# A state-space layer and an attention layer on one core: the first input stretch, and when group 0's y is made

## The chip, the cores and the metric

The kernel runs on one core of a Trainium2 chip. The metric is the device time of one execution in microseconds; before the change it is 840.81 us, the median of three runs (840.78 to 840.98). The engines are PE (matrix products, with the weight loads as PEld), DVE (vector), ACT (scalar functions and casts), POOL (not used here beyond four constants) and SP, whose queue issues nearly all loads.

## The reference, cut to what matters

Two layers with residuals and a final norm, on 512 tokens of width 1024. The change lies in the first layer, the state-space mixer:

```python
proj = u @ in_w                      # u = rms_norm(x); 1024 -> 2048 (z) + 4096 (x, B, C) + 32 (dt)
xbc = silu(causal_depthwise_conv(xbc, conv_w, conv_b))
dt = softplus(dt_raw + dt_bias)
a = dt * (-exp(a_log))
y = ssd_chunked(xs * dt, a, b_in, c_out)     # 8 groups of 4 heads, chunks of 128 tokens
y = y + d_skip * xs
y = gated_group_rms_norm(y, z, norm_w, 8)
return y @ out_w
```

The scan of one group and chunk (t, s are tokens of the chunk) is

```python
cb = C B^T ;  y_diag = (cb * exp(a_cum[t] - a_cum[s]), causal) @ xdt
states = B^T (decay_to_end * xdt), carried from chunk to chunk
y_off = exp(a_cum) * (C @ entering_state)
```

The second layer is latent attention with 16 heads. It is not touched.

## The kernel before, in words

Channels lie on the partitions and the 512 tokens along the free side. Every fp32 operand of a large product is split into a high part and the rest (whi and wlo for weights, vh and vl or ah and al for activations), and a product is three passes: vh with whi, vl with whi, vh with wlo. One projection tile (128 output channels) takes 8 input tiles x 3 = 24 matmuls of 128x512. ACT casts the high part (L272, L398, L311), DVE subtracts it for the rest (L273, L402, L312).

A weight tile is 512 KB. It is loaded on SP's queue into one of two raw buffers (L263), and split into one of three whi and three wlo buffers; the order of the tiles is a list (wq), and a load is issued as soon as its raw buffer is free.

The first layer projects for each of 8 groups six tiles in the order B, C, x0, x1, z0, z1. The projections of group g+1 run on PE while the scan of group g is fed in between. The generator ssm_in yields a cost after every six matmuls and one more at the end of a tile (6 x 0.216 = 1.296 each); `sched` adds these up and calls a piece of other work as soon as the sum reaches the piece's number. The tables S0P, SU, P0 (group 0), P1 (groups 1 to 7) and GN hold these numbers, and PE's order is the order of these calls. On the other engines a scheduler sets the order when the program is built.

The steps that the prediction names:

- *First stretch.* The input x comes in eight tiles (L376), the first two weight tiles in four quarters each between them (L381). B and C of group 0 run in step (gemm2, L300): for each input tile three matmuls of B and three of C. Input is not yet normed there: products use x times the norm's weight, and the norm's factor (rr) is applied to the results.
- *The norm of the input* (norm0, sumsq, L342 to L357, L223, L322 to L324): squares on ACT, sums on DVE, sqh and sql, two products with ones (pssq), logarithm, exponential, and three DVE steps to rr.
- *dt* (ssm_dt): 16 products (L495, L496); the product with rr (d, L500) and four transposes (L504); softplus by a series on DVE; then the second half: cumulative sum by a product (L540), its copy acT (L544) and exponential to DRAM (ac_d, ea_d), transposes of acT (L553), and two more products (L558, L559).
- *The scan of a group* (class SSD): lexp loads four L tiles, broadcast from ac_d (L627), and takes their exponentials; cb (L71 to L81), x for each half (L89 to L94, xdt and xw), states (L105 to L113), y (L123 to L148: loads of E from ea_d, products yo at L130 and yd at L138, and eight DVE steps).
- *The norm of y* (gnorm, sumsq again): for group g it is called in the projections of group g+2, at GN.
- *Convolution and SiLU* of B, C, x0, x1 (L606 to L613): per tile one ACT step and three DVE steps.

Of the kernel before, what the change touches and what calls it, by code (L numbers as in the profile page):

```python
# [50 lines left out]
OA = 8  # L51
SQ = 2


# [97 lines left out]
class Net:  # L152
# [113 lines left out]
    def split_weight(self, raw, cuts=()):  # L266
# [28 lines left out]
    def gemm2(self, ps, ws, xh, xl, ks):  # L295
        seqs = [self.passes(w, xh, xl, ks) for w in ws]
        for k in range(ks):
            for p, seq in zip(ps, seqs):
                for i in range(3 * k, 3 * k + 3):
                    self.nc.tensor.matmul(p, seq[i][0], seq[i][1], start=i == 0, stop=i == 3 * ks - 1)  # L300
            yield 6 * 0.216

# [34 lines left out]
    def sumsq(self, tiles, n, pstag, pool=None, tags=("r0", "rt", "rr"), after=None):  # L337
        nc = self.nc
        acc = None
        for x in tiles:  # L340
# [19 lines left out]
    def ssm(self):  # L360
# [9 lines left out]
        self.link(self.head, [ld])  # L370
        self.phase, self.group = "E", [self.head]
        raws = [self.wraw.tile([P, D], F32, tag="raw", name=self.nm("raw")) for _ in range(2)]
        self.wload = 2
        for k in range(KD):
            x = self.res.tile([P, T], F32, tag="res", name=self.nm("x"))
            nc.sync.dma_start(x[:], t["x"][k])  # L376
            self.xs.append(x)
            if k % 2 == 0:
                s = slice(k * P, (k + 2) * P)
                for i, raw in enumerate(raws):  # L380
                    nc.sync.dma_start(raw[:, s], t["w"][i, :, s])  # L381
        wdt = wk.tile([P, KD, NH], F32, name="wdt", bufs=1)
# [9 lines left out]

        vh, vl = [], []
        ws = [self.split_weight(raw, (256, 512, 768)) for raw in raws]
        for k in range(KD):
            a = self.o16.tile([P, T], F32R, tag="o", name=self.nm("vh"))
            b = self.o16.tile([P, T], F32R, tag="o", name=self.nm("vl"))
            last = nc.scalar.activation(a[:], self.xs[k][:], AF.Copy, scale=nw[:, k:k + 1])  # L398
            if k % 2 == 0:
                for w in ws:  # L400
                    next(w)
            nc.vector.scalar_tensor_tensor(b[:], self.xs[k][:], nw[:, k:k + 1], a[:].bitcast(F32), op0=ALU.mult,  # L402
                                           op1=ALU.subtract)
# [4 lines left out]
        self.wpos = 2  # L408
# [24 lines left out]
        for g in range(NG):  # L433
            ys, q = [], []
            pieces = [] if g == 0 else [(GN, late)]
            if g == 0:
                begin = lambda: q.append(SSD(self, 0, self.lexp(0), ys))
                pieces += [(SU[0] + SU[1] * k, scaled) for k in range(KD)]
                pieces += [(P0[0], step), (P0[1], step), (P0[1] + 0.1, begin)]
                at = P0[2:]  # L440
            else:
                q.append(SSD(self, g, self.lexp(g), ys))
                at = P1
            pieces += [(at[0], lambda: q[0].cb()), (at[1], lambda: q[0].x(0)), (at[2], lambda: q[0].x(1)),
                       (at[3], lambda: q[0].states()), (at[4], lambda: q[0].y())]
            if g + 1 < NG:
# [118 lines left out]
    def ssm_in(self, g, uh, ul, early):  # L565
# [3 lines left out]
        for i, (name, ct) in enumerate((("B", 16 + g), ("C", 24 + g), ("x0", 2 * g), ("x1", 2 * g + 1),  # L569
                                        ("z0", 0), ("z1", 0))):  # L570
            pair = (0, 1) if g == 0 and i < 2 else (4, 5) if g == NG - 1 and i >= 4 else None
            w = None if pair and i == pair[1] else self.weight("w", U_IN + 6 * g + i)
            xh, xl, r = early[:3] if i < early[3] else (uh, ul, None)
# [4 lines left out]
            if pair:  # L578
                if i == pair[0]:
                    two = [ps, self.mm()]  # L580
                    ws = [w, self.weight("w", U_IN + 6 * g + i + 1)]
                    yield from self.gemm2([p[:] for p in two], ws, xh, xl, KD)
# [489 lines left out]
```

## Time and profile before

The profiled execution took 840.15 us, and the span from its first to its last instruction is 838.3 us.

| engine | busy us | share of the span | instructions |
|---|---|---|---|
| PE | 822.8 | 98% | 4260 |
| PEld | 694.8 | 83% | 4260 |
| DVE | 640.2 | 76% | 1226 |
| ACT | 453.5 | 54% | 802 |

The chain that ended last is 91% PE and 5% DVE. A row of a timeline reads: start in us, duration in us, engine, line, operation, output and inputs by the program's names without numbers, shapes, how many equal ones; in brackets the engine's idle time before it and what ended it. Matmuls overlap, so the distance of two starts is what one takes, not its duration. A row of waits reads: who waited, for whom: us in total, times, longest.

### The profile page before, as it was taken

Reading aid. Unit: us, or ns where it says so; the run is one execution under the profiler, and the core shown is the slowest. Engines: PE = TensorE matmul, PEld = TensorE weight load, DVE = VectorE, ACT = ScalarE, POOL = GpSimd, SP = SyncE. Lnnn points to the kernel's source line nnn. Section 1 sums busy time; section 2 is a strip of 40 time slices with the busy share of each in tenths; the row PEclk is TensorE's granted clock in tenths of the full one; section 3 lists DMA queues with packets and bytes.
Section 4 is the critical chain, followed back from the end, with each engine's and each line's share of the span. In section 5 each row is a group of like instructions: output and inputs, shape, how many; then the busy total and the mean of one; then the engine's idle time right before and its main releaser. Section 6 shows DMA issues by size and latency. Waiting matters only on the chain.

```text
span 838.3 us, 11586 instructions
## 1 busy us (share of the span) xinstructions
PE 822.8 (98%) x4260; PEld 694.8 (83%) x4260; DVE 640.2 (76%) x1226; ACT 453.5 (54%) x802; POOL 0.2 (0%) x4
## 2 busy tenths in 40 slices
PE   7999999999999999999999999999999999999996
PEld 5887888888888888888888888888888888888885
DVE  7899898979788979776564887786767869675544
ACT  7567755545565657333354664456547557554233
POOL 0000000000000000000000000000000000000000
PEclk9999999999999999999999999999999999999999
DMA  6354543434242424323225242222221224331212
GB/s 227 102 186 145 153 150 106 147 101 128 98 151 76 151 87 137 121 95 101 90 86 176 79 129 64 77 65 73 73 64 56 89 75 157 100 100 53 92 59 100
DMA packets 35112, 90.55 MB, mean 108 GB/s; under 512 B 4784, under 2 KB 6320, under 8 KB 35056
## 3 DMA queue, kind: packets, MB, share of 16 engines
q1 hardware_dynamic: 34336, 88.77, 32.9%
q10 hardware_dynamic: 720, 1.05, 0.3%
q8 instruction: 33, 0.54, 0.3%
q14 instruction: 23, 0.19, 0.1%
HBM read 83.12 MB, written 4.33 MB: 104 GB/s over the span
## 4 chain that ended last, share of the span: by engine, by line
PE 91%; DVE 5%; DMA 2%; ACT 1%; issue 1%; SPq 0%; DVEq 0%; ACTq 0%
PE mm L291 54%; PE ot L942 11%; PE s L794 5%; PE mm L300 4%; PE po L836 4%; PE mm L774 3%; PE pt L818 2%; PE yd L138 2%; PE yd L291 1%; PE aux L130 1%; PE aux L105 1%; DMA x<-in_x_dram 1%; PE aux L77 1%; PE aux L89 1%; DMA L<-ac_d 1%; DVE wlo L273 1%
## 5 line engine op out<-in xcount | busy, mean ns | idle before, releaser
L272 ACT CAST whi<-raw 128x1024 fp32r<-128x1024 f32 (+3 forms) x132 | 127.0, 965 | 214.7 <-PE mm L291 177.4
L273 DVE TENSOR_TENSOR wlo<-raw,whi 128x1024 fp32r<-128x1024 f32 (+3 forms) x132 | 146.8, 1115 | 56.1 <-ACT whi L272 55.8
L291 PE MATMUL mm<-ah,whi 128*128 128x512 f32 x384 | 153.9, 401 | 0.0
L291 PE MATMUL mm<-ah,wlo 128*128 128x512 f32 x384 | 150.1, 391 | 0.4 <-DVE wlo L273 0.4
L291 PE MATMUL mm<-al,whi 128*128 128x512 f32 x384 | 149.8, 390 | 0.0
L291 PE MATMUL mm<-vh,whi 128*128 128x512 f32 x224 | 89.6, 400 | 0.9 <-ACT whi L272 0.9
L291 PE MATMUL mm<-vh,wlo 128*128 128x512 f32 x224 | 87.8, 392 | 0.7 <-DVE wlo L273 0.7
L291 PE MATMUL mm<-vl,whi 128*128 128x512 f32 x224 | 87.5, 391 | 0.0
L291 PEld LDWEIGHTS mm<-ah,wlo 128*128 128x128 f32 x384 | 72.1, 188 | 16.0 <-DVE wlo L273 0.8
L291 PEld LDWEIGHTS mm<-ah,whi 128*128 128x128 f32 x384 | 72.2, 188 | 15.5 <-issue 1.4
L291 PEld LDWEIGHTS mm<-al,whi 128*128 128x128 f32 x384 | 72.2, 188 | 14.4 <-DVE al L312 0.3
L942 PE MATMUL ot<-whi,ah 128*128 128x512 f32 (+1 forms) x136 | 52.3, 384 | 0.0
L942 PE MATMUL ot<-whi,al 128*128 128x512 f32 (+1 forms) x136 | 51.4, 378 | 0.0
L942 PE MATMUL ot<-wlo,ah 128*128 128x512 f32 (+1 forms) x136 | 51.4, 378 | 0.0
L291 PEld LDWEIGHTS mm<-vh,wlo 128*128 128x128 f32 x224 | 42.0, 188 | 10.8 <-DVE wlo L273 1.5
L291 PEld LDWEIGHTS mm<-vh,whi 128*128 128x128 f32 x224 | 42.1, 188 | 9.2 <-ACT whi L272 1.1
L223 ACT ACTIVATE p<-p,st 128x128 f32<-128x128 f32 (+1 forms) x64 | 36.1, 564 | 25.1 <-DVE st L806 25.0
L291 PEld LDWEIGHTS mm<-vl,whi 128*128 128x128 f32 x224 | 42.2, 188 | 7.2
L822 ACT CAST ph<-pt 128x512 fp32r<-128x512 f32 (+1 forms) x64 | 26.5, 422 | 33.2 <-PE pt L818 32.8
L291 PE MATMUL mm<-ch,whi 128*128 128x512 f32 x104 | 42.6, 409 | 0.0
L291 PE MATMUL mm<-ch,wlo 128*128 128x512 f32 x104 | 40.8, 392 | 0.0
L291 PE MATMUL mm<-cl,whi 128*128 128x512 f32 x104 | 40.7, 392 | 0.0
(225 smaller groups left out, 1642.6 us busy)
## 6 DMA issues: line engine op xcount, KB each, us to landing
raw<-in_w_dram SPq DMA_DIRECT2D x100, 512.0 KB, 3.3
L<-ac_d SPq DMA_DIRECT2D x32, 256.0 KB, 3.8
E<-ea_d SPq DMA_DIRECT2D x32, 128.0 KB, 3.3
raw<-in_ua_dram SPq DMA_DIRECT2D x8, 512.0 KB, 3.3
raw<-in_ub_dram SPq DMA_DIRECT2D x8, 320.0 KB, 2.9
x<-in_x_dram SPq DMA_DIRECT2D x8, 256.0 KB, 4.3
res<-in_x_dram SPq DMA_DIRECT2D x8, 256.0 KB, 3.3
hd<-ht SPq DMA_DIRECT2D x8, 256.0 KB, 2.3
```

What stands on the lines that cost most here:

```text
L138: nc.tensor.matmul(yd[64 * h:64 * h + 64, s], self.xdt[j][:, c, h, :], self.L[2 * j + h][:, s], start=True, stop=True)
L223: i = self.nc.scalar.activation(out, in_, func, **k)
L272: nc.scalar.copy(hi[:, a:b], raw[:, a:b])
L273: nc.vector.tensor_tensor(lo[:, a:b], raw[:, a:b], hi[:, a:b].bitcast(F32), op=ALU.subtract)
L291: self.nc.tensor.matmul(ps, a, b, start=i == 0, stop=i == len(seq) - 1)
L300: self.nc.tensor.matmul(p, seq[i][0], seq[i][1], start=i == 0, stop=i == 3 * ks - 1)
L774: nc.tensor.matmul(ps[:, c2 * 256:(c2 + 1) * 256], a, b, start=i == 0, stop=i == 5)
L794: nc.tensor.matmul(ps[:, :n], x[:, s], y[:, :n], start=k == 0, stop=k == 4)
L818: nc.tensor.transpose(pt[:, (b - kb) * P:(b - kb + 1) * P], probs[h][b][:, kb * P:(kb + 1) * P], self.ident)
L822: nc.scalar.copy(ph[:, :n], pt[:, :n])
L836: nc.tensor.matmul(po[:, kb * P:], x, y, start=kb == 0 and k == 0, stop=kb == NCH - 1 and k == 2)
L942: nc.tensor.matmul(ps[:, a:b], x, y, start=start and i == 0, stop=stop and i == 5)
```

## The change

Four things change.

1. Ahead of everything PE multiplies a tile of zeros by itself eight times (WARM = 8).
2. x0 of group 0 joins B and C in the first stretch: three weight tiles are loaded in quarters between the input tiles, split by split_first, and gemm2 makes nine matmuls for each input tile. The third raw tile lies in two buffers of the pool of ah and al. The squares of the norm are tied to the input tiles three places on, so that they run inside the stretch.
3. S0P: dt's first products, the norm and the flush come right behind the stretch, and dt's transposes behind 12 matmuls of x1 (21.9). P0: dt's second half at 10.4 and 11.2 instead of 6.0 and 6.8, and cb, x0, x1 and states of group 0 later.
4. Group 0's y is no longer called in group 0, but at PL = 5.0 in group 1; group 1's own scan starts (lexp) at 5.1, and its pieces follow a table of their own, PM. GN stays.

```diff
-S0P = (13.82, 14.2, 15.4, 15.6, 17.62)
+S0P = (15.5, 15.51, 15.52, 15.53, 21.9)
 SU = (0.64, 1.42)
-P0 = (6.0, 6.8, 11.91, 15.25, 17.25, 24.88, 34.5)
+P0 = (10.4, 11.2, 16.4, 19.7, 21.7, 29.4)
+PL = 5.0
+PM = (11.0, 12.4, 13.8, 20.0, 26.0)
 P1 = (1.0, 2.4, 3.8, 12.0, 18.2)
 GN = 16.84
...
+WARM = 8
...
+    def split_first(self, raw):
+        nc = self.nc
+        hi = self.whi.tile([P, D], F32R, tag="hi", name=self.nm("whi"))
+        lo = self.wlo.tile([P, D], F32R, tag="lo", name=self.nm("wlo"))
+        for k, part in enumerate(raw):
+            s = slice(2 * k * P, 2 * (k + 1) * P)
+            nc.scalar.copy(hi[:, s], part)
+            nc.vector.tensor_tensor(lo[:, s], part, hi[:, s].bitcast(F32), op=ALU.subtract)
+            yield
+        yield hi, lo
...
-            yield 6 * 0.216
+            yield 3 * len(ws) * 0.216
...
-                self.link(i, [after])
+                self.link(i, [after[k]])
...
+        idle = wk.tile([P, P], F32, name="idle", bufs=1)
+        nc.vector.memset(idle[:], 0.0)
+        pw = aux()
+        for _ in range(WARM):
+            nc.tensor.matmul(pw[:, :P], idle[:], idle[:], start=True, stop=True)
...
-        self.wload = 2
+        raws = [[raw[:, 2 * k * P:2 * (k + 1) * P] for k in range(KD // 2)] for raw in raws]
+        third = [self.act.tile([P, T], F32, tag=g, name=self.nm("raw")) for g in ("ah", "al")]
+        raws.append([third[k // 2][:, (k % 2) * 2 * P:(k % 2 + 1) * 2 * P] for k in range(KD // 2)])
+        self.wload = 3
...
-            pss = self.sumsq([x[:] for x in self.xs], D, "aux", after=last)
+            pss = self.sumsq([x[:] for x in self.xs], D, "aux", after=[marks[min(k + 3, KD - 1)] for k in range(KD)])
...
+            begin = lambda g=g, q=q, ys=ys: q.append(SSD(self, g, self.lexp(g), ys))
             if g == 0:
-                begin = lambda: q.append(SSD(self, 0, self.lexp(0), ys))
                 pieces += [(SU[0] + SU[1] * k, scaled) for k in range(KD)]
                 pieces += [(P0[0], step), (P0[1], step), (P0[1] + 0.1, begin)]
                 at = P0[2:]
+                first = q
+            elif g == 1:
+                pieces += [(PL, lambda: first[0].y()), (PL + 0.1, begin)]
+                at = PM
             else:
-                q.append(SSD(self, g, self.lexp(g), ys))
+                begin()
                 at = P1
...
-                       (at[3], lambda: q[0].states()), (at[4], lambda: q[0].y())]
+                       (at[3], lambda: q[0].states())]
+            if g:
+                pieces.append((at[4], lambda: q[0].y()))
...
-            pair = (0, 1) if g == 0 and i < 2 else (4, 5) if g == NG - 1 and i >= 4 else None
+            pair = (0, 1, 2) if g == 0 and i < 3 else (4, 5) if g == NG - 1 and i >= 4 else None
```

Three places show how the orders move. The first is ACT behind the first stretch; r is the norm's factor in the making, whi_188 and the like are weight tiles (whi_216 is x1's, whi_381 and whi_455 those of z0 and z1). Before:

```order
L342 ACTIVATE sq_299<-x_119 128x512
L353 CAST sqh_302<-sqa_277 128x512
L272 CAST whi_396<-raw_240 128x1024
L223 ACTIVATE r_54_309<-pssq_306 128x512
L223 ACTIVATE r_54_309<-r_54_309 128x512
L272 CAST whi_434<-raw_394 128x1024
```

Now:

```order
L275 CAST whi_216<-raw_212 128x1024
L367 CAST sqh_341<-sqa_316 128x512
L275 CAST whi_381<-raw_214 128x1024
L275 CAST whi_455<-raw_379 128x1024
L226 ACTIVATE r_56_348<-pssq_345 128x512
L226 ACTIVATE r_56_348<-r_56_348 128x512
```

Three weight casts stand ahead of r now, the last of them behind a later load; before, one stood between sqh and r.

The second place is dt's second half on PE, in the last tile of the group. Before:

```order
L540 MATMUL aux_579<-con,a_389 128x128 x4
L291 MATMUL mm_572<-vh_146,whi_506 128x512
L291 MATMUL mm_572<-vl_147,whi_506 128x512
L291 MATMUL mm_572<-vh_146,wlo_507 128x512
L291 MATMUL mm_572<-vh_154,whi_506 128x512
L291 MATMUL mm_572<-vl_155,whi_506 128x512
L291 MATMUL mm_572<-vh_154,wlo_507 128x512
L553 MATMUL aux_605<-ident,acT 128x128 x4
L558 MATMUL aux_612<-da,con 128x128
```

Now:

```order
L305 MATMUL mm_649<-vl_164,whi_589 128x512
L305 MATMUL mm_649<-vh_163,wlo_590 128x512
L568 MATMUL aux_656<-con,a_429 128x128 x4
L581 MATMUL aux_676<-ident,acT 128x128 x4
L586 MATMUL aux_683<-da,con 128x128
L587 MATMUL aux_683<-da,con 128x128
L305 MATMUL mm_649<-vh_167,whi_589 128x512
```

The transposes of acT follow the cumulative sum directly; six matmuls stood between.

The third place is DVE up to the norm of group 0's y (sqa is the sum of squares, sql the rest that the norm's second product reads; cb, L, xdt and xw are group 1's scan, B, C and x convolution steps of group 2). Before, the last rows up to sql:

```order
L81 TENSOR_TENSOR L_934<-L_934,cb_973 128x512
L92 TENSOR_TENSOR xdt_1004<-aux_999,dt 128x512
L610 SCALAR_TENSOR_TENSOR B_1013<-mm_955,cols,B_1013 128x511
L94 TENSOR_TENSOR xw_948<-xdt_1004,dec 128x3x128
L610 SCALAR_TENSOR_TENSOR B_1013<-mm_955,cols,B_1013 128x510
L273 TENSOR_TENSOR wlo_1057<-raw_1018,whi_1056 128x1024
L610 SCALAR_TENSOR_TENSOR B_1013<-mm_955,cols,B_1013 128x509
L347 TENSOR_SCALAR sqa_1118<-sq_1116,eps_1119 128x512
L349 TENSOR_TENSOR sqa_1118<-sqa_1118,sq_1122 128x512
L273 TENSOR_TENSOR wlo_1106<-raw_1054,whi_1105 128x1024
L610 SCALAR_TENSOR_TENSOR C_1049<-mm_1024,cols,C_1049 128x511
L354 TENSOR_TENSOR sql_1126<-sqa_1118,sqh_1125 128x512
```

Now:

```order
L95 TENSOR_TENSOR xdt_1097<-aux_1092,dt 128x512
L97 TENSOR_TENSOR xw_1005<-xdt_1083,dec 128x3x128
L97 TENSOR_TENSOR xw_1005<-xdt_1097,dec 128x3x128
L276 TENSOR_TENSOR wlo_1114<-raw_1042,whi_1113 128x1024
L638 SCALAR_TENSOR_TENSOR x_196_1106<-mm_1048,cols,x_196_1106 128x511
L361 TENSOR_SCALAR sqa_1126<-sq_1124,eps_1127 128x512
L638 SCALAR_TENSOR_TENSOR x_196_1106<-mm_1048,cols,x_196_1106 128x510
L363 TENSOR_TENSOR sqa_1126<-sqa_1126,sq_1130 128x512
L638 SCALAR_TENSOR_TENSOR x_196_1106<-mm_1048,cols,x_196_1106 128x509
L276 TENSOR_TENSOR wlo_1189<-raw_1111,whi_1188 128x1024
L368 TENSOR_TENSOR sql_1134<-sqa_1126,sqh_1133 128x512
```

All of group 1's L, xdt and xw still stand ahead of the sums, as before; new ahead of sql are the convolution steps of x0 and two more of C. The eight steps of group 0's y, which are the first of this list in both programs, stand in the same place relative to it. On PE the norm's first product stands 78 large matmuls, the states and group 1's cb and x behind group 0's y before, and 54 and group 1's cb and x now.

More of the change, by code (lines that the diff above doesn't have):

```diff
@@ L339, in sumsq @@
         acc = None
-        for x in tiles:
+        for k, x in enumerate(tiles):
             sq = self.nrm.tile([P, T], F32, tag="sq", name=self.nm("sq"), bufs=SQ)
@@ L380, in ssm @@
                 for i, raw in enumerate(raws):
[L381 removed]
+                    nc.sync.dma_start(raw[k // 2], t["w"][i, :, s])
         wdt = wk.tile([P, KD, NH], F32, name="wdt", bufs=1)
@@ L391, in ssm @@
         nc.vector.tensor_copy(self.onesr[:], self.ones)
-        vh, vl = [], []
-        ws = [self.split_weight(raw, (256, 512, 768)) for raw in raws]
+        vh, vl, marks = [], [], []
+        ws = [self.split_first(raw) for raw in raws]
         for k in range(KD):
@@ L397, in ssm @@
             b = self.o16.tile([P, T], F32R, tag="o", name=self.nm("vl"))
-            last = nc.scalar.activation(a[:], self.xs[k][:], AF.Copy, scale=nw[:, k:k + 1])
+            marks.append(nc.scalar.activation(a[:], self.xs[k][:], AF.Copy, scale=nw[:, k:k + 1]))
             if k % 2 == 0:
@@ L570, in ssm_in @@
                                         ("z0", 0), ("z1", 0))):
-            pair = (0, 1) if g == 0 and i < 2 else (4, 5) if g == NG - 1 and i >= 4 else None
-            w = None if pair and i == pair[1] else self.weight("w", U_IN + 6 * g + i)
+            pair = (0, 1, 2) if g == 0 and i < 3 else (4, 5) if g == NG - 1 and i >= 4 else None
+            w = None if pair and i != pair[0] else self.weight("w", U_IN + 6 * g + i)
             xh, xl, r = early[:3] if i < early[3] else (uh, ul, None)
@@ L579, in ssm_in @@
                 if i == pair[0]:
-                    two = [ps, self.mm()]
-                    ws = [w, self.weight("w", U_IN + 6 * g + i + 1)]
+                    two = [ps] + [self.mm() for _ in pair[1:]]
+                    ws = [w] + [self.weight("w", U_IN + 6 * g + k) for k in pair[1:]]
                     yield from self.gemm2([p[:] for p in two], ws, xh, xl, KD)
```

2 lines of the change are left out of this document (1 added, 1 removed).

## The prediction

> **What bounds the kernel now.** I read the page first, then the waits of the tensor engine (PE), then its timeline where it waits, then the vector engine (DVE) and scalar engine (ACT) at those places. The page's first line and its chain of waits:
>
> ```profile
> span 838.3 us, 11586 instructions
> PE 91%; DVE 5%; DMA 2%; ACT 1%; issue 1%; SPq 0%; DVEq 0%; ACTq 0%
> ```
>
> The chain that ended last is PE's own queue, so a change is worth what it takes from or adds to PE's waits. These are all of them that the trace lists over the whole span (engine, line, what it waited for: us in total, times, longest):
>
> ```profile
> PE mm L300 <- ACT whi L272: 4.8, 1, 4.8
> PE mm L291 <- DVE wlo L273: 1.0, 3, 0.5
> PE aux L105 <- DVE xw L94: 0.9, 1, 0.9
> PE mm L291 <- ACT whi L272: 0.9, 2, 0.7
> PE aux L504 <- DVE d L500: 0.2, 1, 0.2
> ```
>
> After the start there are 3.0 us of waits in 838, nearly all of them in the first 82 us. What else is lost lies in the pace of the first matmuls (PE's timeline: start us, us long):
>
> ```profile
> 4.77 0.80 PE L300 MATMUL mm<-vh,whi 128*128 128x512 f32 x1 [4.77 <-ACT whi L272]
> ...
> 8.42 0.63 PE L300 MATMUL mm<-vh,wlo 128*128 128x512 f32 x1
> 8.84 0.56 PE L300 MATMUL mm<-vh,whi 128*128 128x512 f32 x1
> 9.24 0.39 PE L300 MATMUL mm<-vl,whi 128*128 128x512 f32 x1
> ...
> 17.64 0.39 PE L300 MATMUL mm<-vh,wlo 128*128 128x512 f32 x1
> 18.69 0.50 PE L291 MATMUL mm<-vh,whi 128*128 128x512 f32 x1 [0.66 <-ACT whi L272]
> ...
> 20.99 0.39 PE L495 MATMUL aux<-vh,w 128*128 128x512 f32 x1
> ...
> 35.48 0.39 PE L291 MATMUL yd<-vh,whi 128*128 128x512 f32 x1
> ```
>
> From 9.24 (the 11th of the 48 products of B and C) to 17.64 (the 48th) a step is 8.40/37 = 0.227 us. Up to 8.84 it is 0.42. The granted clock does not show this (window, its length, PE busy, granted clock, DMA share, GB/s):
>
> ```profile
> 4.00:9.00 5.00, 4.23 (x10) 1.00 0.92 310
> ```
>
> So ten steps from 4.77 to 9.24 take 4.47 us where 2.27 would do: 2.2 us lost. The seven steps from 17.64 to 20.99 take 3.35 instead of 1.59: 1.8 us, the wait for x0's weight.
>
> **The change, part by part.** I compare PE's place at equal work done.
>
> *Zero products.* Eight fp32 products of 128x128. Four such products (L540 below) take 0.81 us at the full pace, 0.20 each; at the slow pace 0.42/0.227 of that, 0.37, so eight take 3.0 us. The memset of their operand is DVE's first:
>
> ```profile
> 0.80 0.12 DVE L331 MEMSET eps<- 128x1 f32 x3 [0.80 <-PEq L1063]
> ```
>
> From about 1.1 us, with 0.2 for the wider memset and the handover, they are over by 4.1 (4.5 if each takes a whole 0.42), before the first real product at 4.77. What hides them is the wait for the first input; without that cover they would cost 3.0. I take them to bring the full pace by about 8 us at the latest, since the old run needed 4.4 us of activity (4.77 to 9.2).
>
> *Three tiles in step.* PE now has 9 products for each of the 8 input tiles (2.04 us), 72 in all. SP issues one more 128 KB load ahead of the second input tile and three more later; 512 KB in all, as x0's separate load goes. In the old run the second tile set the pace at the start:
>
> ```profile
> 2.10 0.91 SPq L376 DMA_DIRECT2D x<-in_x_dram x2
> ...
> 6.22 0.72 ACT L398 ACTIVATE vh<-x,nw 128x512 fp32r<-128x512 f32 x1 [0.63 <-DMA x<-in_x_dram]
> ...
> 6.97 1.64 DVE L402 SCALAR_TENSOR_TENSOR vl<-x,nw,vh 128x512 fp32r<-128x512 f32 x2 [0.93 <-ACT vh L398]
> ```
>
> One issue is 0.46, so the tile lands at 6.2 + 0.46 = 6.65; vh 0.72 and vl 0.8 later it is 8.2, and product 11 (the first with that vl) starts at 8.3. The 62 products from there end at 8.3 + 62 x 0.227 = 22.4. Later tiles cost nothing: the last x, issued 1.8 us later for its four extra loads ahead, is needed only at 22.4 - 2.0. The old run stood at 20.99 with 54 products done, so 72 would have been reached at 25.1: this part gains 2.7 us. The squares and their sums, moved in between, are hidden behind 2.04 us a tile; per pair DVE has about 4.0 us against PE's 4.08 (an estimate from rows shown here: two vl at 0.75, three quarters of a wlo at 0.4, two sums at 0.66).
>
> *The norm and dt's transposes.* This is where the gain goes. Old chain, from the norm's second product to the transposes of dt:
>
> ```profile
> 24.88 0.39 PE L357 MATMUL pssq<-sql,onesr 128*128 128x512 f32 x1
> ```
> ```profile
> 25.31 0.60 ACT L223 ACTIVATE r<-pssq 128x512 f32<-128x512 f32 x1 [0.67 <-PE pssq L357]
> ```
> ```profile
> 28.78 0.69 DVE L500 TENSOR_TENSOR d<-aux,rr 128x512 f32<-128x512 f32 x1
> ```
> ```profile
> 29.53 0.66 PE L504 MATMUL aux<-ident,d 128*128 128x128 f32 x4 [0.16 <-DVE d L500]
> ```
>
> From the logarithm (25.31) to d's end (29.47) are 4.16 us; 18 products covered them, and PE waited 0.3. Now 12 products (2.7 us) stand there, and on ACT the cast of z1's weight (whi_455) stands ahead of the logarithm. That weight's load needs x1's raw buffer free, so x1's cast and subtraction done, and the cast needs the first tile's whi, which PE reads until product 65. The prices:
>
> ```profile
> 17.61 1.03 ACT L272 CAST whi<-raw 128x1024 fp32r<-128x1024 f32 x1
> ```
> ```profile
> 18.67 1.23 DVE L273 TENSOR_TENSOR wlo<-raw,whi 128x1024 fp32r<-128x1024 f32 x1
> ```
> ```profile
> raw<-in_w_dram SPq DMA_DIRECT2D x100, 512.0 KB, 3.3
> ```
>
> Product 65 starts at 22.4 - 8 x 0.227 = 20.6 and is done at 21.0; cast to 22.05, subtraction to 23.3, load landed at 26.65 (27.15 where the load beside it slows it by 0.5), cast to 27.65 (28.15). The logarithm follows there, d ends 4.16 later, the transposes start at 31.85 to 32.35, where PE stands ready at 22.4 + 30 x 0.227 = 29.2: a wait of 2.7 to 3.1 us. Behind it are 12 products fewer than in the old run, where 5.95 us lay between transposes (29.53) and z0 (35.48); so z0 starts at 32.1 + 5.95 - 2.72 = 35.3. Against 35.48 that is **-0.15** (-0.4 to +0.1; +0.8 if the slow pace stays to 9.2 as in the old run, rival 2).
>
> *dt's second half and group 0's scan.*
>
> ```profile
> 53.16 1.05 PE L540 MATMUL aux<-con,a 128*128 128x128 f32 x8
> 53.97 0.48 PE L291 MATMUL mm<-vh,whi 128*128 128x512 f32 x1
> ...
> 78.69 1.56 PE L105 MATMUL aux<-xw,BT 128*128 128x256 f32 x6 [0.87 <-DVE xw L94]
> ```
> ```profile
> 54.41 0.58 ACT L544 COPY acT<-aux 128x512 f32<-128x512 f32 x1
> ```
>
> The cumulative sum and the transposes of its copy now stand next to each other, since both due times fall into one step of the schedule; six products stood between. PE must wait for product and copy: 1.05 + 0.58 + two handovers of 0.05, less the 0.81 of issue: 0.9 us at least. To the states product it was 25.5 us, with a wait of 0.9 at its end for xw, which hangs on the same dt and the L loads; this chain (copy, ac_d, L, xw) keeps its length, but 84 instead of 90 products cover it. So the old wait comes back 1.36 us longer less what is waited at the transposes. Low end 0 (the chain is shorter by the old wait), high end +1.9 (1.36 and half a us of DVE work that is now ahead); the old 0.5 behind the states (wlo) may go. I take **+1.1**, near the plain count of 1.36.
>
> *Group 0's y in group 1.* y's products move from before group 1 to behind its first tile, and the norm of y (GN) stays where it was. Old run:
>
> ```profile
> 86.25 1.50 PE L130 MATMUL aux<-C,S 128*128 128x128 f32 x12
> ...
> 89.58 0.50 PE L291 MATMUL mm<-ah,whi 128*128 128x512 f32 x1
> ...
> 105.51 1.46 PE L105 MATMUL aux<-xw,BT 128*128 128x256 f32 x6
> 106.62 0.58 PE L291 MATMUL mm<-ah,whi 128*128 128x512 f32 x1
> ...
> 110.91 0.39 PE L356 MATMUL pssq<-sqh,onesr 128*128 128x512 f32 x1
> ```
> ```profile
> 87.63 1.01 DVE L144 TENSOR_TENSOR E<-aux,E 128x384 f32<-128x384 f32 x2
> ...
> 97.10 0.88 DVE L634 TENSOR_SCALAR L<-L,ac 128x128 f32<-128x128 f32 x4 [2.84 <-DMA L<-ac_d]
> ...
> 107.86 0.75 DVE L610 SCALAR_TENSOR_TENSOR C<-mm,cols,C 128x511 f32<-128x511 f32 x1
> 108.52 0.68 DVE L354 TENSOR_TENSOR sql<-sqa,sqh 128x512 fp32r<-128x512 f32 x1
> ```
>
> PE had 24.7 us from y's first product (86.25) to the norm's (110.91), and DVE's list from E to sql took 87.63 to 109.20, 21.6 us, of which 2.84 + 0.2 were waits: 18.5 of work, done 1.7 us before PE came. Now PE has 54 instead of 78 products there and no states product: 24.7 - 24 x 0.227 - 1.2 = 18.0 us. DVE's list is the same and five convolution steps longer (two of C, three of x0; 0.66 each, 107.86 to 108.52): 21.8 us. It can't start before the first yo is done, about 0.95 after y's first product. So sql ends 22.75 after it, and the norm's second product, due at 18.25, waits 4.5; sqa, sqh and sql stand behind cb, L and xw on DVE, so no order in time helps. DVE's own waits come on top: 0 to 3.0 as in the old run. By its list it gets to L some 7.4 us after y's first product, and in the old run L came 10.85 after it; but y's rows interleave, and I take 1.5. **+6.0** (4.5 to 7.5). Moving E's four loads costs nothing: they stay right behind the L loads on SP. What waits behind the norm's products on PE is all of group 2's projections; nothing earlier in the queue can fill in.
>
> *Sum:* -0.15 + 1.1 + 6.0 = +6.95 us. On the profiled execution, 840.15 with a span of 838.3, that is 847.1 and 845.25; on the median of 840.81 it is **847.7**. Behind 130 us nothing in the order changes and PE has no wait to swallow it.
>
> **Rivals.**
> 1. *Faster: DVE keeps ahead and the early gain stays.* If z1's weight lands early enough that the logarithm is not delayed, and DVE's list of group 0 finishes before the norm, 2.7 + 0.4 of the first stretch stay: about 837.7. It decides at the norm of group 0: wait below 2 us. For it: 3.9 us of early loss are really there. Against: both waits follow from order and prices.
> 2. *The zero products don't bring the pace.* Then the first nine products run at 0.42 to 8.6 and the slow pace lasts to 9.2: product 11 starts at 9.0 and the first stretch ends 0.7 later, 848.4. For it: 0.4 us of idleness lies between the zero products and the first real one. [...]
> 3. *No change.* DVE's list is early enough at the norm of group 0, but the transposes and dt cost as summed: +0.95, 841.8. It needs yo ready 4.5 us earlier on DVE than PE delivers it.
> 4. *The backlog carries on.* DVE has 3.3 us more to do by the norm and is then late again at group 2's x1 or states, by as much as the old wait of 0.9 twice: +2, 849.7. For it: its list had only 1.7 us to spare before. Against: PE's wait of 6 us gives it time to catch up.
>
> **How the numbers follow.** Forecast 0.62; rival 1 0.07; rival 2 0.12; rival 3 0.06; rival 4 0.13. The bounds of the terms are -0.4 + 0 + 4.5 = 4.1 (844.9) and 0.8 + 1.9 + 7.5 = 10.2 (851.0); the range is 844.2 to 851.0 and leaves out rivals 1 and 3 and a few of the rest. Within 0.2% (1.7 us, about what can be told from no change) is rival 3: 0.06; faster 0.07; slower 0.87.
>
> **What would show it.** Steps of 0.227 by 8.3 us and dt's first product near 22.4; a wait of about 3 us at dt's transposes for d; 0.9 or more at the transposes of acT; and the largest, 4.5 to 7 us, at the norm's products around 112 us, for sqh and then sql. I am wrong if that last wait is under 2 us, or if z0 starts before 33 us.

## The result, and the profile after

The changed kernel takes 850.69 us (median of four executions, 848.23 to 850.73) against 840.89 us of the kernel before beside it (840.78 to 841.21): a ratio of 1.0109, with a 95% interval of 1.0090 to 1.0127. It is slower by 9.8 us, where 6.95 were forecast. The profiled execution took 850.68 us with a span of 848.9.

The page of the changed kernel, its first line, the shares of the chain that ended last, and the granted clock in 40 slices:

```profile
span 848.9 us, 11632 instructions
...
PEclk9999989999999999999999999999999999999999
...
PE 87%; DVE 9%; DMA 2%; ACT 1%; issue 1%; SPq 0%; ACTq 0%; DVEq 0%
```

PE's share of the chain fell from 91 to 87%, DVE's rose from 5 to 9%. The sixth slice of the clock (106 to 127 us) reads 8, where the kernel before had a 9 in all of them. PE's waits (who waited, for what: us in total, times, longest):

```profile
PE pssq L370 <- ACT sqh L367: 5.1, 1, 5.1
PE aux L532 <- issue: 2.5, 1, 2.5
PE aux L108 <- DVE xw L97: 2.3, 1, 2.3
...
PE pssq L371 <- DVE sql L368: 0.9, 1, 0.9
PE aux L581 <- ACT acT L572: 0.7, 1, 0.7
```

These are the places that the prediction named: the norm of y (L370, L371), dt's transposes (L532), the states (L108), the transposes of acT (L581). PE's timeline of the first stretch:

```profile
6.76 0.44 PE L314 MATMUL mm<-vl,whi 128*128 128x512 f32 x1
7.04 0.39 PE L314 MATMUL mm<-vh,wlo 128*128 128x512 f32 x1
...
8.55 0.50 PE L314 MATMUL mm<-vl,whi 128*128 128x512 f32 x1 [0.20 <-DVE vl L424]
...
22.74 0.39 PE L523 MATMUL aux<-vh,w 128*128 128x512 f32 x1
...
32.22 0.63 PE L532 MATMUL aux<-ident,d 128*128 128x128 f32 x4 [2.48 <-issue]
...
35.44 0.39 PE L305 MATMUL yd<-vh,whi 128*128 128x512 f32 x1
```

The full pace is there from 7.04 (before: 9.24), dt's first product comes at 22.74 with 18 products more done than the old 20.99, and the transposes wait 2.48 us, so that z0 starts at 35.44 against 35.48 (the profile names no releaser for that wait; d, their operand, ends at 32.12 on DVE). Up to there the change has brought nothing and cost nothing. PE's timeline at the states and at the norm of group 0:

```profile
82.27 0.39 PE L305 MATMUL mm<-ah,wlo 128*128 128x512 f32 x1
84.96 2.52 PE L108 MATMUL aux<-xw,BT 128*128 128x256 f32 x6 [2.30 <-DVE xw L97]
86.91 0.99 PE L305 MATMUL mm<-ah,whi 128*128 128x512 f32 x1
...
88.89 0.39 PE L305 MATMUL mm<-al,whi 128*128 128x512 f32 x1
...
94.81 1.50 PE L133 MATMUL aux<-C,S 128*128 128x128 f32 x12
...
112.48 0.39 PE L305 MATMUL mm<-ah,wlo 128*128 128x512 f32 x1
117.94 0.80 PE L370 MATMUL pssq<-sqh,onesr 128*128 128x512 f32 x1 [5.07 <-ACT sqh L367]
119.68 0.79 PE L371 MATMUL pssq<-sql,onesr 128*128 128x512 f32 x1 [0.95 <-DVE sql L368]
120.27 0.63 PE L305 MATMUL mm<-ah,whi 128*128 128x512 f32 x1
...
122.83 0.44 PE L305 MATMUL mm<-ah,whi 128*128 128x512 f32 x1
...
162.54 0.39 PE L370 MATMUL pssq<-sqh,onesr 128*128 128x512 f32 x1
```

Behind both waits the products run at the slow pace of the start. The states' six products last 2.52 us (1.56 in the kernel before). From their first to the fifth product behind them, at 88.89, are 3.93 us, where the same takes 2.32 at full pace (84.58 to 86.90 in the first experiment below): 1.6 us lost. The seven steps from 119.68 to 122.83 take 3.15 us, where 0.34 for the first and 0.23 for each of the others, as in that experiment, make 1.7: 1.4 us lost. (The expectations below were worked out with 2.0 for the first and 1.3 for the second.) The windows view of the same kernel shows why (window, its length, busy time of PE, PEld, DVE, ACT, POOL with counts, granted clock, DMA share, GB/s):

```profile
81.95:85.36 3.41, 1.11 (x6) 0.65 (x5) 3.41 (x6) 2.62 (x4) 0.00 (x0) 1.00 0.00 0
85.36:88.78 3.42, 3.42 (x10) 2.69 (x9) 2.67 (x5) 0.00 (x0) 0.00 (x0) 0.50 0.49 150
112.67:116.08 3.41, 0.20 (x1) 0.00 (x0) 3.41 (x7) 0.38 (x1) 0.00 (x0) 1.00 0.03 5
116.08:119.50 3.42, 0.80 (x1) 0.29 (x1) 3.42 (x5) 0.62 (x1) 0.00 (x0) 0.50 0.42 149
119.50:122.91 3.41, 3.23 (x8) 2.55 (x9) 1.20 (x3) 2.35 (x3) 0.00 (x0) 0.50 0.49 154
```

The granted clock is 0.50 in whole pieces of 3.41 us, whose edges all lie on one grid: from 88.78 to 116.08 are eight pieces of 3.41. A piece in which PE was busy for 1.11 of 3.41 us is followed by one at half the clock.

At equal work the ledger is this. y's first product comes at 94.81 with one tile of 24 products (5.44 us) ahead of it that stood behind it before; 86.25 + 5.44 = 91.69, so the stretch from z0 to there costs 3.1 us. The next point at which both kernels have done the same is the norm of group 1's y, the 162.54 above against

```profile
151.03 0.39 PE L356 MATMUL pssq<-sqh,onesr 128*128 128x512 f32 x1
```

in the kernel before: 11.5 us, of which 8.4 fall behind y's first product. DVE's rows from y to the norm say what the norm waits for, from the first E to the last step, sql:

```profile
95.68 0.56 DVE L147 TENSOR_TENSOR E<-aux,E 128x384 f32<-128x384 f32 x1 [1.26 <-PE aux L133]
...
104.61 0.29 DVE L662 TENSOR_SCALAR L<-L,ac 128x128 f32<-128x128 f32 x1 [2.42 <-DMA L<-ac_d]
...
118.94 0.68 DVE L368 TENSOR_TENSOR sql<-sqa,sqh 128x512 fp32r<-128x512 f32 x1
```

They take 23.94 us, of which 2.42 are the wait for group 1's L loads; the rest is 21.5 us of work. Nothing more is lost behind the norm of group 1's y; PE's last product starts 11.3 us later than before, and the last write ends 0.7 sooner behind it, which makes the 10.6 us between the spans.

### The profile page after: what moved, and what is told of

Read it like the earlier page. It is cut to its first block, busy times and chain, and to the rows that moved or that the text cites. A ratio compares the mean times of both kernels' runs of the same rounds, so it can differ in the third digit from the quotient of the medians.

```text
span 848.9 us, 11632 instructions
## 1 busy us (share of the span) xinstructions
PE 828.9 (98%) x4276; PEld 700.1 (82%) x4276; DVE 641.4 (76%) x1230; ACT 453.5 (53%) x805; POOL 0.2 (0%) x4
## 3 DMA queue, kind: packets, MB, share of 16 engines
q10 hardware_dynamic: 720, 1.05, 0.3%
## 4 chain that ended last, share of the span: by engine, by line
PE 87%; DVE 9%; DMA 2%; ACT 1%; issue 1%; SPq 0%; ACTq 0%; DVEq 0%
PE mm L305 50%; PE ot L970 10%; PE mm L314 6%; PE s L822 5%; PE po L864 3%; PE mm L802 3%; PE pt L846 2%; PE yd L141 2%; DMA L<-ac_d 2%; PE aux L108 1%; PE aux L133 1%; DVE wlo L276 1%; DVE x L638 1%; PE aux L80 1%; PE aux L92 1%
## 5 line engine op out<-in xcount | busy, mean ns | idle before, releaser
L275 ACT CAST whi<-raw 128x1024 fp32r<-128x1024 f32 (+2 forms) x123 | 123.1, 1002 | 209.9 <-PE mm L305 167.9
L276 DVE TENSOR_TENSOR wlo<-raw,whi 128x1024 fp32r<-128x1024 f32 (+2 forms) x123 | 142.6, 1160 | 64.0 <-ACT whi L275 63.8
L305 PE MATMUL mm<-vh,whi 128*128 128x512 f32 x216 | 86.0, 398 | 0.0
L305 PE MATMUL mm<-vh,wlo 128*128 128x512 f32 x216 | 84.5, 391 | 0.2 <-DVE wlo L276 0.2
L305 PE MATMUL mm<-vl,whi 128*128 128x512 f32 x216 | 84.3, 390 | 0.0
```

Source lines behind the costliest of these rows:

```text
L275: nc.scalar.copy(hi[:, a:b], raw[:, a:b])
L276: nc.vector.tensor_tensor(lo[:, a:b], raw[:, a:b], hi[:, a:b].bitcast(F32), op=ALU.subtract)
L305: self.nc.tensor.matmul(ps, a, b, start=i == 0, stop=i == len(seq) - 1)
```

## The experiments

Each edit is to the changed kernel, except where the kernel before is named.

**PE kept busy in the two long waits.** Zero products ahead of the states' products of group 0 and ahead of the norm's products of its y.

```diff
+FILL_S, FILL_N = 8, 20
...
+        for _ in range(FILL_S if self.g == 0 else 0):
+            nc.tensor.matmul(pp[0][:, :P], net.idle[:], net.idle[:], start=True, stop=True)
...
+        for _ in range(fill):
+            nc.tensor.matmul(ps[:, :P], self.idle[:], self.idle[:], start=True, stop=True)
```

> Changed kernel plus zero products of 128x128 (0.20 us each) on the tensor engine inside its two long waits: 8 ahead of group 0's states product, 20 ahead of the norm's products of group 0. No other order changes; the real products start when their operands are ready, as before. Theory A (the part missing from the forecast is a granted clock that falls after the two waits and stays low for 3.4 and 6.8 us): the two matmul lines stay at the full pace, which saves about 2.0 us after the states and 1.3 us after the norm, and the time is about 847.4 us (850.7 less 3.3), with the 6 us between the products before the norm and its first real product still there. Theory B (the missing part is vector-engine work that is late, and the slow matmuls only fill time that would be waited anyway): the waits grow by what the pace gains, and the time stays within 0.7 us of 850.7. Theory C (the zero products themselves delay real ones): above 851.5.

Measured: 849.35 us (849.24 to 849.53 in three executions, 847.46 in the fourth; the mean granted clock was 0.995 to 0.996 in the three and 0.999 in the fourth). Its timeline:

```profile
82.27 1.95 PE L109 MATMUL aux<-idle 128*128 128x128 f32 x16
84.58 1.56 PE L111 MATMUL aux<-xw,BT 128*128 128x256 f32 x6 [0.36 <-DVE xw L98]
...
86.90 0.39 PE L308 MATMUL mm<-al,whi 128*128 128x512 f32 x1
...
92.81 1.50 PE L136 MATMUL aux<-C,S 128*128 128x128 f32 x12
...
117.76 0.50 PE L376 MATMUL pssq<-sql,onesr 128*128 128x512 f32 x1 [1.24 <-DVE sql L371]
...
146.14 0.63 PE L93 MATMUL aux<-ident,x 128*128 128x128 f32 x4 [0.69 <-DVE cb L83]
```

At the states the real products start 0.4 us earlier than in the changed kernel, last 1.56 us again, and y's first product comes 2.0 us earlier (92.81 for 94.81). That is theory A's time at this place, but 1.6 of it is the pace; the other 0.4 is the earlier start, of which 0.2 lies ahead of dt's transposes already (32.02 for 32.22) and so is no effect of the edit. Behind the norm the clock fell nevertheless:

```profile
115.63:119.04 3.41, 1.78 (x7) 1.25 (x8) 2.08 (x3) 1.05 (x3) 0.00 (x0) 1.00 0.27 71
119.04:122.46 3.42, 3.42 (x10) 2.64 (x9) 2.77 (x5) 3.39 (x5) 0.00 (x0) 0.50 0.22 87
```

The twenty products ended at 115.34, too early: in the piece with the last 1.9 us of waiting PE was busy for 1.78 of 3.41 us, and that was too little. So only one of the two low stretches went, and part of what it gave is waited again at 146.14 for cb, because DVE is now the later one (theory B, for 0.7 us of it). The one execution at 847.46, with a mean clock of 0.999, is theory A's 847.4; its trace was not taken, so that the second half of A is borne out by time and clock alone.

**The norm of group 0's y later.**

```diff
+GN1 = 8.0
...
-            pieces = [] if g == 0 else [(GN, late)]
+            pieces = [] if g == 0 else [(GN + GN1 * (g == 1), late)]
```

> Changed kernel with only the norm of group 0's y put later in group 1, by some 30 products (8 units of the schedule). Theory A (the largest wait is nothing but the position: the norm of y was left where it stood while y moved behind group 1's first tile): the wait of 5.1 + 0.9 us at the norm's products goes, the fall of the clock behind it too (1.3), nothing takes its place: 843.4 us. Theory B (rival 4 of the prediction: the vector engine is behind, and the wait returns at group 2's x1 or states): at least half of the 6 us returns there, 846.5 us or more.

Measured: 841.83 us (839.66 to 844.69), ratio to the kernel before 1.0022 (1.0008 to 1.0035). The wait of 6 us is gone, and at group 2's x1 and states, where theory B had it return, PE does not wait; the only wait behind the norm is one of 0.7 us for half a weight, after 400 us. That is theory A, and rival 4 falls here. The time is under A's number, which kept the low clock behind the states: in this profiled execution it is not there, and the clock fell behind dt's transposes instead:

```profile
28.88:32.29 3.41, 1.01 (x6) 0.58 (x6) 3.31 (x6) 0.05 (x1) 0.00 (x0) 1.00 0.46 154
32.29:35.70 3.41, 3.41 (x11) 2.73 (x10) 3.41 (x7) 2.23 (x3) 0.00 (x0) 0.50 0.00 0
83.49:86.90 3.41, 1.69 (x10) 1.17 (x8) 3.26 (x6) 2.38 (x4) 0.00 (x0) 1.00 0.03 5
```

The same wait of 2.4 us at dt's transposes that the changed kernel bore at full clock lies here within one piece and halves the next; the states' wait of 1.72 us lies within one piece too, but leaves it busy for 1.69 of 3.41 us, and the clock holds. The grid lies elsewhere from trace to trace, and the times of this kernel spread over 5 us. That the spread is the grid's doing is argued from the mean clocks, as only one of these executions was traced: 839.66 and 839.80 at a mean clock of 0.997, 841.75 to 842.81 at 0.996 to 0.997, 843.34 to 844.69 at 0.993 to 0.994.

**The waits that are left, filled.** Norm later, and zero products in the two waits over 1.5 us, ahead of dt's transposes and of the states' products.

```diff
+FILL_S, FILL_D = 7, 10
...
         pt = aux()
+        for _ in range(FILL_D):
+            nc.tensor.matmul(pt[:, :P], self.idle[:], self.idle[:], start=True, stop=True)
```

> As the run with the norm put later, plus zero products in the two waits that are left over 1.5 us: 10 ahead of dt's transposes (2.4 us idle there), 7 ahead of the states product of group 0 (1.7 us idle). Theory A (the spread of that run, 839.7 to 844.7 us, is the granted clock: a window of 3.4 us in which the tensor engine is busy half of the time or less is followed by one at half the clock, and where the windows lie changes from execution to execution): no low clock anywhere before the last few us, and all executions within 0.7 us of 839.7. Theory B (the spread comes from the loads or from something else that waits): the spread stays 3 us or more, and the median within 1 us of 841.8.

Measured: 839.90 us (839.04 to 841.00 in ten executions). No piece at half the clock is found before the last products, and the spread went from 5.0 to 2.0 us, not to the 0.7 expected. Theory A for the larger part. What is left is another thing: the profiled execution, one of its slowest (840.84), has the transposes 1.0 us later than the run with the norm later,

```profile
32.90 0.66 PE L538 MATMUL aux<-ident,d 128*128 128x128 f32 x4 [1.14 <-DVE d L532]
```

because ACT's squares of the input ended about 1.2 us later (the cast sqh at 23.31 for 22.12). The delay begins at a tile of the input that landed late; in the changed kernel, which has the same first stretch but for the filled wait, ACT takes this tile at 9.45, after a wait of 0.15 us:

```profile
10.62 0.73 ACT L424 ACTIVATE vh<-x,nw 128x512 fp32r<-128x512 f32 x1 [1.56 <-DMA x<-in_x_dram]
```

So theory B's loads make part of the spread that is left.

**Without the zero products.** WARM = 0.

> Changed kernel without the eight zero products at the start. Theory A (they bring the full pace about 2.2 us earlier, near 7.0 instead of 9.2, but 10 products at 0.42 against 0.227 in that time count only where the input does not set the pace): dt's first product 0.7 to 1.0 us later than 22.74, and the end as much later, about 851.5. Rival 1 (the full pace comes at the same moment without them): 850.7. Rival 2 (the wait at dt's transposes absorbs what is lost): dt's first product later, z0 not, 850.7.

Measured: 856.17 us (853.22 to 859.92), 5.5 us more than the changed kernel, where at most 1.0 was expected. In its trace the full pace comes at 9.75 us and dt's first product 0.9 us later than in the changed kernel (23.61), as theory A had it. But the span is 6.2 us longer (855.1): 1.1 at dt's transposes (33.29), 1.6 up to the transposes of acT (62.98), as the clock falls behind dt's transposes too, 1.0 more up to the norm (121.58), and 2.7 up to the norm of group 1's y (168.92), where the clock stays low for three pieces instead of two and a wait of 1.3 us for cb follows; 0.2 comes back at the end. The pieces at the norm:

```profile
118.96:122.38 3.42, 0.79 (x1) 0.28 (x1) 3.42 (x6) 0.62 (x1) 0.00 (x0) 0.50 0.42 153
122.38:125.79 3.41, 2.46 (x6) 1.98 (x7) 1.23 (x3) 1.58 (x3) 0.00 (x0) 0.50 0.44 154
125.79:129.20 3.41, 3.41 (x10) 2.63 (x9) 3.15 (x5) 2.60 (x4) 0.00 (x0) 0.50 0.00 0
```

2.46 us of work in a piece did not bring the full clock back; it came after a piece that was full. No theory of mine had this. In this trace dt's transposes wait within one piece (busy for 0.73 of 3.41 us), which they did not in the changed kernel. Why all four executions lost at least 2.5 us, and not only the traced one, stays open.

**The zero products alone, in the kernel before.**

```diff
+WARM = 8
...
+        for _ in range(WARM):
+            nc.tensor.matmul(pw[:, :P], idle[:], idle[:], start=True, stop=True)
```

> Kernel before with nothing but eight zero products of 128x128 ahead of its first load. Theory A (in the two-tile order what the earlier pace gains is waited again for x0's weight, which came at 18.69 and 19.7 whatever the pace was): the 48th product starts 1 us earlier or more, dt's first product stays within 0.3 us of 20.99, and the time is 840.8. Rival (the pace alone is worth its 2.2 us, or the half of it that falls before 7 us): 838.6 to 839.7.

Measured: 839.81 us against 840.44, ratio 0.9995 (0.9986 to 1.0004). The executions lie in two groups, 838.95 to 840.02 (six) and 840.90 to 841.28 (four). The profiled one is of the upper group. Its 48th product starts 0.7 us earlier (16.91 for 17.64), where theory A had 1 or more, and the wait for x0's weight grew from 0.66 to 1.44 us, as theory A had it. With it the clock fell, which no theory had, and dt's first product comes at 21.70, outside A's 0.3 us around 20.99. No single wait in that piece is longer than 1.44 us; a second one, of 0.53 us, is for the second half of the weight (wlo).

```profile
16.79:20.21 3.42, 1.46 (x6) 0.60 (x5) 3.17 (x5) 3.26 (x6) 0.00 (x0) 1.00 0.19 77
20.21:23.62 3.41, 3.41 (x9) 2.64 (x9) 2.76 (x4) 1.51 (x3) 0.00 (x0) 0.50 0.73 190
```

The lower group is about 1.1 us faster than the kernel before, which the rival gives and A does not; where that 1.1 comes from stays open, as no trace of that group was taken.

**dt and group 0's scan back at their old positions.**

```diff
-P0 = (10.4, 11.2, 16.4, 19.7, 21.7, 29.4)
+P0 = (6.0, 6.8, 11.91, 15.25, 17.25, 24.88)
```

> Changed kernel with dt's second half and group 0's scan at the positions that they had before (six pieces, 4.4 to 4.5 units earlier); first stretch and the late y stay as changed. Theory A (the prediction's: the two pieces of dt in one step cost 0.9 or more, and six products less of cover cost the rest): no wait at the transposes of acT, the states wait 0.9 instead of 2.3 us, no low clock behind the states: 846.5 to 848.0. Theory B (the vector engine takes the copy of the cumulative sum 9 us after it is there, behind scaled inputs and convolutions, so that its list sets when the states' operand is ready wherever the pieces stand): the wait at the states stays at 2.0 or more, the time is 849.5 to 851.

Measured: 850.19 us (849.66 to 851.22). Its timeline at the states and y:

```profile
78.76 1.56 PE L108 MATMUL aux<-xw,BT 128*128 128x256 f32 x6 [1.23 <-DVE xw L97]
...
91.72 1.50 PE L133 MATMUL aux<-C,S 128*128 128x128 f32 x12
...
116.11 0.79 PE L370 MATMUL pssq<-sqh,onesr 128*128 128x512 f32 x1 [6.33 <-ACT sqh L367]
```

The wait at the states falls to 1.23 us, that at acT's transposes to none, no low clock follows, and y's first product comes 3.1 us earlier: level with the kernel before (91.69 as worked out above). So the later place of dt and the scan costs 3.1 us there, the low clock behind the states included, as theory A says in kind. But the time is theory B's: the wait at the norm grows from 5.07 to 6.33, the clock is low for three pieces from 112.26 to 122.50, and 0.5 us are left of the 3.1. The gain ahead of the largest wait went into that wait (1.3 us) and the longer low clock around it.

**Group 0's y back in group 0.**

```diff
-                first = q
-            elif g == 1:
-                pieces += [(PL, lambda: first[0].y()), (PL + 0.1, begin)]
-                at = PM
+                pieces.append((39.0, lambda q=q: q[0].y()))
```

> Changed kernel with only group 0's y put back to the end of group 0, ahead of group 1's first tile; the states, dt and the first stretch stay as changed. Theory A (the move of y makes the norm's wait and nothing else of size): the 6.0 us at the norm's products and the low clock behind them (1.3) go; y's products may wait up to 1.2 us for the states' sums, since no tile stands between them now: 843.4 to 844.6 where a low clock follows the states as in the changed kernel, 841.5 to 842.5 where not. Rival (the early y costs elsewhere what the late norm costs, so that the wait only changes its place): 848 or more.

Measured: 842.97 us (840.82 to 844.64), ratio 1.0025 (1.0014 to 1.0035). The wait at the norm's products is gone: theory A, though the median lies between its two ranges and the fastest execution under both. The edit also takes PL and PM away, so that group 1's scan starts at once again and goes by P1. The profiled execution is the fastest and has no low clock before its end; its waits are dt's transposes (2.5), the states (1.5) and the states' sums (0.9).

**A version from the single results.** The norm later, dt's transposes two steps later in the first stretch, and cb, x0 and x1 of group 0 half a step and its states one step later. (The expectation calls the former cumulative products; dt's cumulative sum stays at 10.4.)

```diff
-S0P = (15.5, 15.51, 15.52, 15.53, 21.9)
+S0P = (15.5, 15.51, 15.52, 15.53, 24.4)
...
-P0 = (10.4, 11.2, 16.4, 19.7, 21.7, 29.4)
+P0 = (10.4, 11.2, 17.05, 20.35, 22.35, 30.7)
...
+GN1 = 8.0
...
-            pieces = [] if g == 0 else [(GN, late)]
+            pieces = [] if g == 0 else [(GN + GN1 * (g == 1), late)]
```

> Changed kernel with the norm of group 0's y later (as in the run above), dt's transposes two steps later in the first stretch (12 more products ahead of them, which cover the 2.4 us that they wait), and group 0's cumulative products and states half a step and one step later. Theory A (the transposes' wait and part of the states' are a matter of position; each wait left is under 1.4 us, so no low clock follows): 2 to 2.5 us under the undisturbed executions of the run with the norm later, so 837.2 to 838. Theory B (the vector engine's list sets the end of group 0's scan, so a wait that is covered early comes back at the second weight half or at the states): 839.5 to 842.

Measured: 837.93 us (837.37 to 838.54), ratio 0.9965 (0.9951 to 0.9979) to the kernel before: faster than both kernels (0.35% under the kernel before), and its five executions lie within 1.2 us. Its waits:

```profile
PE aux L582 <- ACT acT L573: 1.6, 1, 1.6
...
PE aux L109 <- DVE xw L98: 1.0, 1, 1.0
```

The wait at dt's transposes is gone, the largest one left is 1.6 us, over the 1.4 that theory A allowed, and the clock is full up to the last products. The time is theory A's; what B feared is seen at acT's transposes alone, which wait longer (1.6 for 0.7).

**The same without the zero products.** WARM = 0.

> The combined version (norm of y later, dt's transposes two steps later, products and states of group 0 a little later) without the eight zero products. Theory A (they bring the full pace 2.2 to 3 us earlier, worth 0.8 to 1.1 us to the first stretch, and with no wait over 1.7 us behind it nothing multiplies the loss as it did in the changed kernel, where taking them away cost 5.5): 838.7 to 839.2 us, executions within 2 us of each other. Rival 1 (the vector engine's list sets the end of group 0's scan, so the start's loss is waited there anyway): 837.9. Rival 2 (without them waits grow over half a window and the clock falls as in the changed kernel): 841 or more.

Measured: 838.56 us (838.34 to 839.23 in nine executions; a tenth took 2942 us, for a reason that no trace shows, and is left out), ratio 0.9978 (0.9968 to 0.9988). This is nearest to theory A, 0.1 us under its range: dt's first products come 1.1 us later, the end 0.6 to 0.7 by the medians and spans. The intervals of the two ratios overlap, so the 0.6 is not clear of rival 1's nothing. The same edit cost 5.5 us in the changed kernel, where long waits stood behind it.

## Why the prediction was right, and where its sum was short

- **The first stretch** (forecast -0.15): -0.04. Full pace at 7.04 (by 8 at the latest), product 11 at 8.55 (8.3), dt's first product at 22.74 (22.4), the transposes at 32.22 (31.85 to 32.35), their wait 2.48 (2.7 to 3.1). The zero products took 3.78 us (1.05 to 4.83), not 3.0, and so ended just as the first real product started (4.82), not 0.7 us ahead of it: that they cost nothing was closer than the sum had it. Rival 2 is out: without the zero products the slow pace lasts to 9.75. The clock record of the trace begins with the first full clock: at 6.85 us in the changed kernel and at 9.19 in the kernel before. The steps of 0.23 us begin between 5.90 and 7.04 in the eight traces with zero products and between 9.24 and 9.91 in the three without. In the seven that also have the three-tile order, product 11 starts at 8.09 to 8.55 all the same, in five of them after a wait of 0.20 to 0.29 us for its vl, so there the input sets the pace and not the clock.
- **dt's second half and group 0's scan** (forecast +1.1, 0 to +1.9): +3.1, outside its bounds. 1.6 of it is the slow pace behind the states' wait; the 1.5 that is left lies inside them (with PE kept busy there, y's first product is 1.1 behind, 92.81 against 91.69, of which the first stretch of that trace gave 0.2). Of the two parts, acT's transposes waited 0.68 (0.9 forecast). What I had not worked out there is DVE's list. In the changed kernel DVE copies the result of those transposes at 70.34, 9.4 us after it is there (60.29 + 0.66); in the kernel before at 61.22, 5.2 us after (55.43 + 0.60):

```profile
70.34 0.28 DVE L583 COPY ac<-aux 128x128 f32<-128x128 f32 x1
```
```profile
61.22 0.28 DVE L555 COPY ac<-aux 128x128 f32<-128x128 f32 x1
```

- **Group 0's y in group 1** (forecast +6.0, 4.5 to 7.5): waits of 5.07 + 0.95 = 6.02. From y's first product to the norm's second are 24.87 us (119.68 - 94.81), forecast 22.75 + 1.5 = 24.25; DVE waited 2.42 us for the L loads in between, 0.9 more than I took, and had 21.5 us of work, 0.3 less than the 21.8 of the sum. By starts the two products cost 6.7, as the product ahead of the long wait lasts 0.39 us and the one behind it 0.80, where a step is 0.23. Putting the norm later removes the wait with nothing else moved, and putting y back removes it as well: it is the place of y against its norm that makes it.
- **The sum** lacked a term: it priced each wait at its own length, and nothing in it stood for the clock that falls behind a wait. That term measured 1.6 us behind the states and 1.4 behind the norm. 6.95 + 3.0 is about 10.0, against 10.6 between the spans; what is left is the three terms themselves, about 1.5 larger without the clock than forecast, less the 0.9 by which the end of the program came sooner. The measured 850.69 lies inside the range of 844.2 to 851.0 by 0.3 us. The upper end was the sum of all upper bounds, 0.8 of it for rival 2, which did not come, so that it was luck that the range still held without the missing term. I had read the clock as a matter of the start alone, since the trace of before shows no fall up to its last microseconds: its longest wait behind the start is 0.9 us.
- **The rivals.** 1 and 3 needed a short wait at the norm. 4 is not seen in the changed kernel (after 165 us PE waits 0.2 us in all), but such a wait does occur in two other traces, for cb at group 2's x: 0.7 us in the run with PE kept busy and 1.3 us without the zero products. Its time, 849.7, lies nearer to the measured one than the forecast of 847.7 does, but not for its reason.

## To carry to other kernels

When a forecast makes PE wait, price the wait and then the clock behind it: here waits that filled more than half of a 3.4 us piece cost 1.4 to 1.6 us more, depending on where they fell. A spread of several us between executions of one kernel went with it (5.0 us, and 2.0 with the waits filled). Work that is moved later should take its readers with it: the norm of y, left where it was, made 8 of the 11.5 us, and one number gave them back. Where a larger wait followed, an early gain was mostly lost in it (0.5 of 3.1 us were left with the scan put back), so the largest wait is to be removed first.

## What the runs showed of the hardware that I had not expected

The granted clock has two values in these traces, 1.00 and 0.50, and changes only on a grid of 3.41 us that is fixed within an execution (in the changed kernel from the fall at 85.36 to the one at 846.53 are 223 pieces) and lies elsewhere from trace to trace (an edge at 30.75 in the changed kernel, at 28.88 in the run with the norm later). The pieces by how much of them PE was busy at full clock, in the profiled executions:

| PE busy in the piece | kernel, start of the piece in us | clock of the next piece |
|---|---|---|
| 0.00 | changed, 843.12, and before, 831.80 (behind the last products) | 0.50 |
| 0.06, 0.33 | changed, 112.67 and 81.95 | 0.50 |
| 0.13, 0.21, 0.29 | without zero products, 115.55, 30.22, 84.83 | 0.50 |
| 0.27 | scan back, 108.84 | 0.50 |
| 0.30 | norm later, 28.88 | 0.50 |
| 0.43 | before with zero products, 16.79 | 0.50 |
| 0.52 | PE kept busy, 115.63 | 0.50 |
| 0.50 | norm later, 83.49, and PE kept busy, 30.30 | 1.00 |
| 0.52 | combined version, 55.40, and scan back, 30.34 | 1.00 |
| 0.55, 0.57 | y back, 30.48 and 81.68 | 1.00 |
| 0.57 | changed, 30.75 | 1.00 |
| 0.60, 0.61 | changed, 839.70, and before, 828.39 (the last products) | 1.00 |

In these traces the border lies near one half: up to 0.43 the clock fell each time, from 0.55 on it held each time, and of the five pieces between (0.50 to 0.52) four held and one fell, so the busy time alone does not settle those. At half clock a piece with 0.23, 0.59 or 0.72 busy kept the clock low, one with 0.95 or 1.00 raised it. The start follows the same grid: in the changed kernel 85.36 less 23 pieces is 6.9, and the steps turn from 0.43 to 0.23 between 6.76 and 7.04; the views show a granted clock of 1.00 ahead of that all the same, as the record begins only there, so that at the start the distance of the matmuls has to tell.

The length of a single wait did not decide: waits of 2.30 us (changed, the states) and 2.40 us (norm later, dt's transposes) were followed by half the clock, one of 2.48 us at dt's transposes (changed, and y back) was not, and in the kernel before with zero products two of 1.44 and 0.53 us in one piece were.
